# Hybrid attention and pooling block: numerator halves made further ahead, gate multiply and value-matrix product moved to later steps, PSUM banks shared

## The chip, the cores and the metric

One core of a Trainium2 chip runs the whole program. The metric is device time in microseconds (us) of one execution; the time before is the median of three runs. TensorE is called PE here (PEld is its weight load), VectorE DVE, ScalarE ACT, GpSimd POOL, and SP is SyncE, which issues the DMAs.

## What is computed

The reference is one layer of a hybrid block over 2048 latent tokens and 256 context tokens of width 1024. Cut to what matters here:

```python
h = _rms(x, norm_g) * (1 + scale) + shift          # hc likewise from ctx
u, uc = h @ w_in, hc @ w_in
q, k, v = _mla_qkv(u, ...)                          # 4 heads; rank-128 latent for keys and values
attn = softmax(q @ [kc, k].T * scale) @ [vc, v]     # 2048 queries, 2304 keys
br_a = silu(gate_a) * attn
br_p = silu(gate_p) * multiscale_pool(u, ...)
x_new = x + gate * (concat(br_a, br_p) @ w_out)
```

## The kernel before

The kernel works in three stages. A start-up and feature stage (to about 550 us) makes the modulated input, its projections, queries, keys, gates and the pooling branch. The attention stage (about 520 to 1100 us) follows. The output projection (L1012 to L1056) ends the kernel. Operands of matmuls are split in two halves, a rounded one and the rest, so that three products of halves stand for one product in full precision; `split` (L94) does so with an ACT copy and a subtraction.

**Attention.** The queries of a head come in blocks of 512, 16 blocks in all (`blocks`, L741), and a block is two row pairs p of 256 queries, 32 pairs. `scores(p, i)` (L757) handles 128 rows, i = 0 or 1: five chunks of keys (four of 512 in "A" banks, one of 256 in an "X" bank), five matmuls each; DVE takes the maximum of each chunk (L775), then ACT makes the exponentials (L793), a batch of five, and DVE transposes them in 32 by 32 squares into a W buffer (L796). `shuffle(p)` (L803) finishes the transpose with 16 DMAs on SP from that buffer to another W buffer (`PT[p]`). `pv(p)` (L845) takes nine steps: for each, `halves` (L850) makes the two halves of 256 numerators by 256 keys from `PT[p]`, ACT the first (L853), POOL the second (DVE for some; L855), in an M buffer, and `pv_mm` (L817) multiplies them with the latent values on PE (L821), six matmuls. Halves are made two steps ahead inside a pair; at a pair's beginning the first three are made at once. The last pair to end scores, 31, goes another way (`pv_last`, L829), with transposes on PE.

A block's two outputs lie in one "O" bank (L824). `latents(n)` (L892) copies it, split in two, to T buffers; `finish(n)` (L899) multiplies these with the value matrix (L903), multiplies with the gate (L905) and stores the branch (L908). `norm(n)` (L868) makes the reciprocals of the row sums: a PE transpose, two DMAs to DRAM (L879, L881), a DMA back that spreads them over the partitions (L884), the load of the gate (L886), and on POOL the product of the two (L887).

**What sets the order.** `attn` (L953) steps through the scores, ten steps a pair, and by a fixed rate lets `pv_all` (L929) do a step whenever it is due; LAG is 22 score steps:

```python
                    while done < (gc - LAG) * 9 / PER:
                        next(pg)
                        done += 1
```

So nine value steps go with ten score steps, and pair p's first value step stands in the program 13 score steps after the end of its scores. In `pv_all`, `norm(n)` comes at the start of a block's second pair, `latents` at its end, `finish` after step 2 of the next pair. From this program order a scheduler lays down a fixed order for each engine and for the SP queue, by priced durations; at run time each engine works through its list in order and waits at semaphores.

**Buffers.** SBUF buffers are given out by tag (L34): W 5, B 8, M 6, T 10, U 5. In the attention stage two W buffers hold transposes, two the shuffled numerators; M buffers hold the queries of the present and the next block, the value matrix and the halves. The query load of the next block (`load_q`, L735, L737), the key loads of the next head at two pairs (`load_k`, L712) and the loads of the output weights at pairs 28 to 30 (`load_wo`, L916) stand on the same SP queue. PSUM has 8 banks: A 5, X 2, O 1 (L78). "O" also serves a start-up sum (L297) and the pooling product (L648); X serves the last score chunk, transposes, `norm` and `finish`.

Of the kernel before, what the change touches and what calls it, by code (L numbers as in the profile page):

```python
# [10 lines left out]
F16 = mybir.dt.float16  # L11
# [13 lines left out]
NJ = NKEY // 128  # L25
# [28 lines left out]


LAG = 22
K_PF = (3, 5)
WO_AT = (1, 5, 11, 12, 12, 12, 13, 13)
CHUNKS = ((0, 512), (512, 512), (1024, 512), (1536, 512), (2048, 256))
# [4 lines left out]
def tile_hybrid_block(ctx: ExitStack, tc: tile.TileContext, x, c, cx, c_ctx, w_mod, b_mod, norm_g,  # L64
# [3 lines left out]
    x, cx, out = x[0], cx[0], out[0]  # L68
# [6 lines left out]
    sm = ctx.enter_context(tc.tile_pool(name="sm", bufs=3))  # L75
    ps = ctx.enter_context(tc.tile_pool(name="ps", bufs=1, space=bass.MemoryType.PSUM))
    dr = ctx.enter_context(tc.tile_pool(name="dr", bufs=1, space=bass.MemoryType.DRAM))
    PBUFS = {"A": 5, "X": 2, "O": 1}  # L78
    uid = [0]

    def nm(s):
# [3 lines left out]
    def st(tag, shape, dt=F32):  # L85
        return sb.tile([128] + list(shape), dt, tag=tag, bufs=BUFS[tag], name=nm(tag))

    def pt(tag, cols=512):
        return ps.tile([128, cols], F32, tag=tag, bufs=PBUFS[tag], name=nm("p" + tag))

# [200 lines left out]
    def mod_sum(b):  # L291

        wm, k0 = wms[b], KPS[b]
        mc = pt("X")
        mcv = mc[:, 0:8].rearrange("p (k s) -> p k s", s=2)
        if k0:
            mp = pt("O")  # L297
            for k in range(k0):
                nc.tensor.matmul(mp[0:2, :], lhsT=scv[:, k, :], rhs=wm[k // 2][:, k % 2, :], start=(k == 0),
                                 stop=(k == k0 - 1))  # L300
            mrow = st("T", [512])
            nc.scalar.copy(out=mrow[0:2, :], in_=mp[0:2, :])
        for i in range(4):
            if k0:
                nc.tensor.matmul(mcv[:, i, :], lhsT=mrow[0:2, i * 128:(i + 1) * 128], rhs=ident[0:2, 0:2],
                                 start=True, stop=(k0 == KT))
            if k0 < KT:
                nc.tensor.matmul(mcv[:, i, 0:1], lhsT=accs[b][:, i * 128:(i + 1) * 128], rhs=ones,
                                 start=(k0 == 0), stop=True)
        for i, o in ((0, 8), (1, 0)):  # L310
            nc.vector.tensor_copy(out=modc[:, b, 2 * i:2 * i + 2, :],
                                  in_=bmc[:, o + 2 * b:o + 2 * b + 2].unsqueeze(2).broadcast_to([128, 2, 2]))
        if k0 < KT:
            if k0:
                nc.vector.tensor_tensor(out=modc[:, b, :, 1], in0=mcv[:, :, 1], in1=modc[:, b, :, 1], op=ALU.add)
            mod_cols(b, 0, mcv[:, :, 0])
        else:
            for s in range(2):
                mod_cols(b, s, mcv[:, :, s])
# [275 lines left out]
    def feat(b):  # L595
# [6 lines left out]
        for g in range(H):  # L602
# [42 lines left out]
            n0 = a  # L645
            while n0 < e:
                n1 = e if e - n0 <= 512 else n0 + 260
                pp = pt("O")  # L648
                for n, (w, r) in enumerate(((wph, ph), (wph, pl), (wpl, ph))):
                    nc.tensor.matmul(pp[:, 0:n1 - n0], lhsT=w[:, g, :], rhs=r[:, n0:n1],  # L650
                                     start=(n == 0), stop=(n == 2))
                bo = st("T", [512])
                nc.vector.scalar_tensor_tensor(out=bo[:, 0:n1 - n0], in0=pp[:, 0:n1 - n0], scalar=psc[:, g:g + 1],
                                               in1=gp[:, n0 - 8:n1 - 8], op0=ALU.mult, op1=ALU.mult)
                nc.sync.dma_start(out=brd[1, g, :, t0 + n0 - 16:t0 + n1 - 16], in_=bo[:, 0:n1 - n0])
                n0 = n1
# [144 lines left out]
    PT = {}  # L801
# [21 lines left out]

    def out_bank(p):  # L824
        if p // 2 not in O:
            O[p // 2] = pt("O")
        return O[p // 2][:, (p % 2) * 256:(p % 2) * 256 + 256]

    def pv_last(p):  # L829
# [12 lines left out]
            pv_mm(p, o, j2, t)  # L842
            yield

    def pv(p):  # L845
        o = out_bank(p)
        src = PT.pop(p).rearrange("p q i j b -> p (q i) j b")
        ts = []

        def halves(j2):  # L850
            t = st("M", [2, 2, 8, 32], F16)
            s2 = src[:, :, 2 * j2:2 * j2 + 2, :].rearrange("p x j b -> p j x b")
            nc.scalar.activation(out=t[:, 0], in_=s2, func=AF.Copy)  # L853
            eng = nc.vector if j2 == 4 or (p == NP - 2 and j2 % 2) else nc.gpsimd
            eng.tensor_tensor(out=t[:, 1], in0=s2, in1=t[:, 0], op=ALU.subtract)  # L855
            ts.append(t)

        for j2 in range(NJ // 2):
            if j2 == 0:
                halves(0)  # L860
                halves(1)
            if j2 + 2 < NJ // 2:
                halves(j2 + 2)
            t = ts.pop(0)
            pv_mm(p, o, j2, t)
            yield

    def norm(n):  # L868

        h, qb = blocks[n]  # L870
        s4 = small(4, "s4")
        for i in range(4):
            nc.vector.reduce_sum(s4[:, i:i + 1], RS[n][i], axis=AX.X)
        nc.vector.reciprocal(out=s4, in_=s4)
        b = pt("X")
        nc.tensor.transpose(b[0:4, 0:128], s4, ident)
        rr = sm.tile([4, 128], F32, tag="rr", bufs=2, name=nm("rr"))
        nc.vector.tensor_copy(out=rr, in_=b[0:4, 0:128])
        nc.sync.dma_start(out=rvd[n].rearrange("(s n i r) -> s i n r", s=2, n=4, i=2)[0],  # L879
                          in_=rr[0:2].rearrange("i (n r) -> i n r", n=4))  # L880
        nc.sync.dma_start(out=rvd[n].rearrange("(s n i r) -> s i n r", s=2, n=4, i=2)[1],  # L881
                          in_=rr[2:4].rearrange("i (n r) -> i n r", n=4))
        rb = st("T", [512])
        nc.sync.dma_start(out=rb, in_=rvd[n].partition_broadcast(128))  # L884
        ga = st("T", [512])
        nc.sync.dma_start(out=ga, in_=gad[h, :, qb * 512:(qb + 1) * 512])  # L886
        nc.gpsimd.tensor_tensor(out=ga.rearrange("p (r n) -> p r n", n=16),  # L887
                                in0=ga.rearrange("p (r n) -> p r n", n=16),
                                in1=rb.rearrange("p (n r) -> p r n", n=16), op=ALU.mult)
        return ga  # L890

    def latents(n):  # L892

        o = O.pop(n)
        ol = [st("T", [512], F32R) for _ in range(2)]
        split(o, *ol)
        return ol
# [29 lines left out]
                yield  # L927

    def pv_all():  # L929
        ol = None  # L930
        for p in range(NP - 2):
            if p % 2:
                gau = norm(p // 2)
            for k, _ in enumerate(pv(p)):
                if k == 2 and ol:
                    finish(p // 2 - 1, ol, gaus)
                    ol = None
                yield
            if p % 2:
                ol, gaus = latents(p // 2), gau  # L940
        gau = norm(NP // 2 - 1)
        for k, _ in enumerate(pv_last(NP - 1)):
            if k == 2:
                finish(NP // 2 - 2, ol, gaus)
            yield
        yield from pv(NP - 2)
        finish(NP // 2 - 1, latents(NP // 2 - 1), gau)

    PER = 10
    WO_PF = (28, 29, 30)  # L950
# [154 lines left out]
```

## Time and profile before

| what | value |
|---|---|
| runs of the kernel before | 1283.88, 1286.53, 1290.29 us; median 1286.53 |
| the profiled execution, its own time | 1288.46 us |
| its span, first to last instruction | 1286.7 us |
| mean granted TensorE clock | 0.984 |
| PE, DVE, ACT, POOL busy | 1212.8, 831.1, 738.5, 562.1 us |

The span is one execution, from its first to its last instruction; times inside the trace count from the span's start. Idle time of an engine stands with what ended it, the releaser. The granted clock is a share of the full 2.4 GHz.

### The profile page before, as it was taken

How to read it: one execution, taken by the hardware profiler on the slowest of the kernel's cores; microseconds unless marked ns; L12 is line 12 of the kernel's file. 1: busy time of each engine (PE TensorE's matmuls, PEld its weight loads, DVE VectorE, ACT ScalarE, POOL GpSimd, SP SyncE). 2: the span in 40 equal slices, each digit the busy share in tenths (PEclk: the TensorE clock that was granted, in tenths of full speed). 3: DMA queues.
4: the chain of work that ended last, by engine and by line, in shares of the span. 5: the costliest groups of instructions: out<-in, count | busy, mean ns of one | idle time of the engine just before them, and what ended most of it. 6: DMA issues, size and time to landing. Idle time of an engine off the chain costs nothing.

```text
span 1286.7 us, 22292 instructions
## 1 busy us (share of the span) xinstructions
PE 1212.8 (94%) x7805; PEld 954.5 (74%) x7805; DVE 831.1 (65%) x1595; ACT 738.5 (57%) x1780; POOL 562.1 (44%) x638
## 2 busy tenths in 40 slices
PE   6799999999999998988999989999899999899998
PEld 3698989989899998755566655666556667688887
DVE  4966654765666555677788887888778887631211
ACT  5575665655575654466777767777667777511000
POOL 3645313524344342025566645654656654332221
PEclk9799999999999999999999999999999999999999
DMA  9446952574446547367877787777777778563321
GB/s 304 149 122 138 228 137 66 130 198 136 94 108 153 113 126 196 90 150 172 199 188 181 182 203 188 182 176 196 185 176 183 179 191 236 194 238 135 115 98 49
DMA packets 208213, 208.66 MB, mean 162 GB/s; under 512 B 92339, under 2 KB 168420, under 8 KB 207974
## 3 DMA queue, kind: packets, MB, share of 16 engines
q1 hardware_dynamic: 208102, 207.25, 62.0%
q8 instruction: 61, 1.00, 0.3%
q14 instruction: 50, 0.41, 0.1%
HBM read 98.50 MB, written 35.56 MB: 104 GB/s over the span
## 4 chain that ended last, share of the span: by engine, by line
PE 70%; DMA 11%; DVE 5%; SPq 5%; ACT 4%; issue 2%; POOL 2%; ACTq 0%; DVEq 0%; POOLq 0%
PE pA L588 17%; PE pA L1028 14%; PE pA L772 14%; PE pO L821 9%; PE pA L244 6%; SPq L811 3%; PE pA L519 2%; POOL M L855 2%; DMA M<-in_w_in_dram 2%; DMA rvd<-rr 2%; ACT M L853 2%; PE pX L772 1%; DMA W<-W 1%; DVE W L796 1%; PE pA L494 1%
## 5 line engine op out<-in xcount | busy, mean ns | idle before, releaser
L855 POOL TENSOR_TENSOR M<-W,M 128x512 f16<-128x512 f32 x244 | 291.3, 1218 | 193.3 <-ACT M L853 193.2
L772 PE MATMUL pA<-B,M 128*128 128x512 f16 x1280 | 303.9, 381 | 7.0 <-ACT T L793 3.6
L588 PE MATMUL pA<-W,B 128*128 128x256 f32 x2304 | 307.3, 287 | 0.1
L588 PEld LDWEIGHTS pA<-W,B 128*128 128x128 f32 x2304 | 290.2, 192 | 3.5 <-issue 0.9
L772 PEld LDWEIGHTS <-M 128*128 128x128 f16 x1600 | 156.4, 98 | 145.6 <-issue 7.3
L821 PE MATMUL pO<-M,B 128*128 128x256 f16 x1728 | 222.1, 276 | 21.2 <-POOL M L855 20.3
L793 ACT ACTIVATE T<-pA,nm,gm 128x512 f32<-128x512 f32 x248 | 189.6, 775 | 62.7 <-DVE nm L781 62.7
L821 PEld LDWEIGHTS <-B 128*128 128x128 f16 x1728 | 168.9, 99 | 71.6 <-issue 31.6
L796 DVE STREAM_TRANSPOSE W<-T 128x512 f32<-128x512 f32 x310 | 197.6, 647 | 25.2 <-ACT T L793 14.3
L853 ACT ACTIVATE M<-W 128x512 f16<-128x512 f32 x279 | 164.7, 632 | 84.3 <-PE pO L821 65.2
L775 DVE TENSOR_REDUCE mx<-pA 128x1 f32<-128x512 f32 x256 | 173.3, 680 | 37.8 <-PE pA L772 36.3
L1028 PE MATMUL pA<-W,B 128*128 128x512 f32 (+1 forms) x792 | 178.7, 386 | 4.8 <-ACT B L96 4.8
L1028 PEld LDWEIGHTS pA<-W,B 128*128 128x128 f32 x792 | 146.0, 189 | 34.2 <-ACT B L96 5.1
L1052 POOL TENSOR_TENSOR M<-T,M 128x512 f32<-128x512 f32 x30 | 38.7, 1294 | 113.6 <-DVE T L1049 109.4
L1049 DVE TENSOR_TENSOR T<-pA,M 128x512 f32<-128x512 f32 (+1 forms) x33 | 22.0, 673 | 101.1 <-PE pA L1028 101.1
L244 PE MATMUL pA<-B,W 128*128 128x448 f32 (+1 forms) x288 | 86.4, 371 | 0.0
L97 DVE TENSOR_TENSOR B<-M,B 128x1024 fp32r<-128x1024 f32 x48 | 61.5, 1282 | 32.1 <-ACT B L96 32.0
L96 ACT ACTIVATE B<-M 128x1024 fp32r<-128x1024 f32 (+2 forms) x53 | 55.3, 1044 | 45.2 <-DMA M<-in_w_in_dram 37.5
L887 POOL TENSOR_TENSOR T<-T,T 128x512 f32<-128x512 f32 x16 | 24.6, 1540 | 82.8 <-DMA T<-gad 49.5
L96 ACT ACTIVATE B<-B 128x2048 fp32r<-128x2048 f32 x8 | 15.3, 1918 | 75.2 <-DMA B<-brd 75.2
L244 PEld LDWEIGHTS pA<-B,W 128*128 128x128 f32 x288 | 54.7, 197 | 4.4 <-DVE T L275 0.9
L244 PE MATMUL pA<-W,W 128*128 128x448 f32 (+1 forms) x144 | 52.9, 369 | 0.0
(193 smaller groups left out, 1513.4 us busy)
## 6 DMA issues: line engine op xcount, KB each, us to landing
W<-W SPq DMA_DIRECT2D x496, 144.0 KB
M<-in_w_in_dram SPq DMA_DIRECT2D x48, 512.0 KB
B<-in_x_dram SPq DMA_DIRECT2D x16, 512.0 KB
B<-brd SPq DMA_DIRECT2D x8, 1024.0 KB
M<-in_x_dram SPq DMA_DIRECT2D x16, 512.0 KB
out_dram<-M SPq DMA_DIRECT2D x15, 512.0 KB
brd<-T SPq DMA_DIRECT2D x24, 256.0 KB
kd<-T SPq DMA_DIRECT2D x36, 128.0 KB
```

The costliest lines, as they stand in the source:

```text
L96: a = nc.scalar.activation(out=hi, in_=src, func=AF.Copy)
L97: (eng or nc.vector).tensor_tensor(out=lo, in0=src, in1=hi if hi.dtype == F16 else hi.bitcast(F32), op=ALU.subtract)
L244: nc.tensor.matmul(p[:, c0:NTOK], lhsT=a[:, kt, k * 128:(k + 1) * 128], rhs=b, start=(kt == 0 and n == 0), stop=(kt == KT - 1 and n == 2))
L588: nc.tensor.matmul(p[:, i * HB:(i + 1) * HB], lhsT=w[:, a, kt, :], rhs=b[:, kt, :], start=(m == 0), stop=(m == 23))
L772: nc.tensor.matmul(b[:, s0:s0 + sn], lhsT=q[:, a, c, p % 2, i], rhs=kt[ki][:, kc, o:o + sn], start=(m == 0), stop=(m == 4))
L775: nc.vector.reduce_max(mx[:, n:n + 1], b[:, :w], axis=AX.X)
L793: nc.scalar.activation(out=e[:, :w], in_=sp[n][:, :w], func=AF.Exp, bias=ng, scale=escale, accum_out=rs[:, n:n + 1])
L796: nc.vector.transpose(TP[p][:, :, i, j0:j1, :].rearrange("p q j b -> p j q b"), e[:, :w].rearrange("p (j q b) -> p j q b", q=4, b=32))
L821: nc.tensor.matmul(o, lhsT=V[0][:, j, a], rhs=t[:, c, jj], start=(j == 0 and m == 0), stop=(j == NJ - 1 and m == 2))
L853: nc.scalar.activation(out=t[:, 0], in_=s2, func=AF.Copy)
L855: eng.tensor_tensor(out=t[:, 1], in0=s2, in1=t[:, 0], op=ALU.subtract)
L1028: nc.tensor.matmul(bank[k, n, c0][:, 0:c1 - c0], lhsT=a[:, kt, k * 128:(k + 1) * 128], rhs=w[:, c, kt % 2, n * 512 + c0:n * 512 + c1], sta ...
```

## The change

Halves no longer use M buffers but a ring of eight slices in one W buffer (the fifth), made across the ends of pairs: at each value step `halves` fills a queue up to six, the present step's and five ahead, as far as `shuffle` of the pair has been issued in the program. The ninth slice holds the spread reciprocals. `norm` is cut in two: the loads stay where they were (at the end of a block's first pair), the multiply with the gate (`gated_norm`) comes after step 4 of the next block's first pair, and `finish` after its step 6 in place of 2. For the last block, `norm` comes after `pv_last(31)`, and its gate multiply at the very end. The O bank is gone; X has three banks, and outputs, the start-up sum and the pooling product take theirs from X.

```diff
+AHEAD, RING = 5, 8
+FIN_AT = (4, 6)
...
-    PBUFS = {"A": 5, "X": 2, "O": 1}
+    PBUFS = {"A": 5, "X": 3}
...
-            mp = pt("O")
+            mp = pt("X")
...
-                pp = pt("O")
+                pp = pt("X")
...
-            O[p // 2] = pt("O")
+            O[p // 2] = pt("X")
...
-    def pv(p):
-        o = out_bank(p)
-        src = PT.pop(p).rearrange("p q i j b -> p (q i) j b")
-        ts = []
-
-        def halves(j2):
-            t = st("M", [2, 2, 8, 32], F16)
-            s2 = src[:, :, 2 * j2:2 * j2 + 2, :].rearrange("p x j b -> p j x b")
+    aux, hq = [], []
+    todo = [(p, j2) for p in range(NP - 1) for j2 in range(NJ // 2)]
+
+    def halves(ahead=AHEAD):
+        while todo and len(hq) < ahead and todo[0][0] in PT:
+            p, j2 = todo.pop(0)
+            if not aux:
+                a = st("W", [4608])
+                aux.extend(a[:, i * 512:(i + 1) * 512] for i in range(9))
+            n = p * (NJ // 2) + j2
+            t = aux[n % RING].bitcast(F16).rearrange("p (c j x b) -> p c j x b", c=2, j=2, x=8)
+            s2 = PT[p].rearrange("p q i j b -> p j (q i) b")[:, 2 * j2:2 * j2 + 2]
             nc.scalar.activation(out=t[:, 0], in_=s2, func=AF.Copy)
             eng = nc.vector if j2 == 4 or (p == NP - 2 and j2 % 2) else nc.gpsimd
             eng.tensor_tensor(out=t[:, 1], in0=s2, in1=t[:, 0], op=ALU.subtract)
-            ts.append(t)
-
+            hq.append((p, j2, t))
+
+    def pv(p):
+        o = out_bank(p)
         for j2 in range(NJ // 2):
-            if j2 == 0:
-                halves(0)
-                halves(1)
-            if j2 + 2 < NJ // 2:
-                halves(j2 + 2)
-            t = ts.pop(0)
+            halves(AHEAD + 1)
+            ph, jh, t = hq.pop(0)
             pv_mm(p, o, j2, t)
             yield
+        PT.pop(p)
...
-        rb = st("T", [512])
+        rb = aux[RING]
         nc.sync.dma_start(out=rb, in_=rvd[n].partition_broadcast(128))
         ga = st("T", [512])
         nc.sync.dma_start(out=ga, in_=gad[h, :, qb * 512:(qb + 1) * 512])
+        return rb, ga
+
+    def gated_norm(rb, ga):
         nc.gpsimd.tensor_tensor(out=ga.rearrange("p (r n) -> p r n", n=16),
...
     def pv_all():
-        ol = None
-        for p in range(NP - 2):
-            if p % 2:
-                gau = norm(p // 2)
-            for k, _ in enumerate(pv(p)):
-                if k == 2 and ol:
-                    finish(p // 2 - 1, ol, gaus)
-                    ol = None
+        last = None
+        for p in [*range(NP - 2), NP - 1, NP - 2]:
+            for k, _ in enumerate(pv_last(p) if p == NP - 1 else pv(p)):
+                if last and k == FIN_AT[0]:
+                    gau = gated_norm(*last[2])
+                if last and k == FIN_AT[1]:
+                    finish(*last[:2], gau)
+                    last = None
                 yield
-            if p % 2:
-                ol, gaus = latents(p // 2), gau
-        gau = norm(NP // 2 - 1)
-        for k, _ in enumerate(pv_last(NP - 1)):
-            if k == 2:
-                finish(NP // 2 - 2, ol, gaus)
-            yield
-        yield from pv(NP - 2)
-        finish(NP // 2 - 1, latents(NP // 2 - 1), gau)
+            if p % 2 == 0 and p < NP - 2 or p == NP - 1:
+                nrm = norm(p // 2)
+            else:
+                last = p // 2, latents(p // 2), nrm
+        finish(*last[:2], gated_norm(*last[2]))
```

## Rows read from the trace of the kernel before

**Rows 1.** The page, busy time, share of the span and instructions of each engine

```profile
PE 1212.8 (94%) x7805; PEld 954.5 (74%) x7805; DVE 831.1 (65%) x1595; ACT 738.5 (57%) x1780; POOL 562.1 (44%) x638
```

**Rows 2.** Stretches: length; PE, PEld, DVE, ACT, POOL busy; PEclk, DMA share, GB/s

```profile
603.00:1055.00 452.00, 428.58 (x2756) 272.68 (x2756) 368.16 (x754) 329.19 (x768) 263.41 (x221) 0.99 0.77 187
...
845.60:878.77 33.17, 32.48 (x212) 20.85 (x212) 27.96 (x59) 25.24 (x60) 20.46 (x18) 1.00 0.77 184
878.77:917.11 38.34, 34.09 (x213) 21.46 (x213) 28.50 (x59) 25.59 (x60) 20.08 (x18) 0.96 0.78 189
```

**Rows 3.** Waits of PE, 550 to 1100 us: us in total, times, longest

```profile
PE pO L821 <- POOL M L855: 20.3, 14, 4.1
PE pX L903 <- ACT T L96: 9.6, 14, 0.7
PE pA L1028 <- ACT B L96: 4.8, 1, 4.8
...
PE pO L821 <- ACT M L853: 0.9, 1, 0.9
```

**Rows 4.** One of five stretches at the lower clock, columns as in rows 2

```profile
904.40:907.81 3.41, 2.99 (x14) 1.92 (x14) 0.00 (x0) 1.24 (x2) 3.41 (x4) 0.50 0.98 230
```

**Rows 5.** Timeline of PE and POOL in the longer block: start, us, instruction, [idle before]

```profile
904.82 2.72 PE L821 MATMUL pO<-M,B 128*128 128x256 f16 x12 [3.56 <-POOL M L855]
...
902.13 1.53 POOL L887 TENSOR_TENSOR T<-T,T 128x512 f32<-128x512 f32 x1 [7.60 <-DMA W<-W]
903.62 5.59 POOL L855 TENSOR_TENSOR M<-W,M 128x512 f16<-128x512 f32 x5
```

**Rows 6.** Timeline of the SP queue in the same block

```profile
888.94 0.59 SPq L712 DMA_DIRECT2D B<-kd  x1
...
890.61 0.36 SPq L881 DMA_DIRECT2D rvd<-rr  x1
896.11 0.34 SPq L884 DMA_DIRECT2D T<-rvd  x1
```

**Rows 7.** Timeline of PE at the end of a block

```profile
841.48 3.44 PE L821 MATMUL pO<-M,B 128*128 128x256 f16 x30
845.60 0.74 PE L903 MATMUL pX<-T,M 128*128 128x512 f32 x2 [0.69 <-ACT T L96]
```

**Rows 8.** Waits of the SP queue, 520 us to the end

```profile
SPq L735 <- PE pO L821: 60.2, 13, 7.1
...
SPq L811 <- POOL M L855: 15.3, 11, 5.6
```

**Rows 9.** Pair 17: last transposes, shuffle, two stretches (as rows 2), first halves

```profile
837.96 1.03 DVE L796 STREAM_TRANSPOSE W<-T 128x512 f32<-128x512 f32 x2
...
844.60 10.74 SPq L811 DMA_DIRECT2D W<-W  x16
...
844.60:858.00 13.40, 12.71 (x83) 8.00 (x82) 11.46 (x23) 11.04 (x28) 5.99 (x6) 1.00 0.91 222
858.00:860.00 2.00, 2.00 (x11) 0.94 (x10) 1.90 (x6) 0.94 (x2) 2.00 (x2) 1.00 0.16 59
...
864.21 1.67 ACT L853 ACTIVATE M<-W 128x512 f16<-128x512 f32 x3
```

**Rows 10.** Pair 17: PE's last score group, first and last exponential of its second batch

```profile
834.00 0.71 PE L772 MATMUL pX<-B,M 128*128 128x256 f16 x5
...
834.28 0.78 ACT L793 ACTIVATE T<-pA,nm,gm 128x512 f32<-128x512 f32 x1 [0.54 <-DVE nm L781]
...
837.32 0.57 ACT L793 ACTIVATE T<-pX,nm,gm 128x256 f32<-128x256 f32 x1
```

**Rows 11.** Timeline of ACT in the tail

```profile
1097.12 1.91 ACT L96 ACTIVATE B<-B 128x2048 fp32r<-128x2048 f32 x1 [5.77 <-DMA B<-brd]
...
1105.10 2.18 ACT L853 ACTIVATE M<-W 128x512 f16<-128x512 f32 x4
```

More of the change, by code (lines that the diff above doesn't have):

```diff
@@ L855, in halves @@
             eng.tensor_tensor(out=t[:, 1], in0=s2, in1=t[:, 0], op=ALU.subtract)
-            ts.append(t)
+            hq.append((p, j2, t))
+    def pv(p):
+        o = out_bank(p)
         for j2 in range(NJ // 2):
-            if j2 == 0:
-                halves(0)
-                halves(1)
-            if j2 + 2 < NJ // 2:
-                halves(j2 + 2)
-            t = ts.pop(0)
+            halves(AHEAD + 1)
+            ph, jh, t = hq.pop(0)
+            assert (ph, jh) == (p, j2)
             pv_mm(p, o, j2, t)
             yield
+        PT.pop(p)
     def norm(n):
```

## The prediction

> **What bounds the kernel now.** I read the page first: TensorE is busy 1212.8 of 1286.7 us, 94%, and no other engine passes 65% [rows 1]. A busy share can mean slow matmuls, so I next took the stretches of the attention stage. From 603 to 1055 us, thirteen blocks of two row pairs, PE is busy 428.58 of 452 us and VectorE, next, 368 [rows 2]. A block without a stall lasts 33.17 us with PE busy 32.48; one with a stall lasts 38.34 with PE busy 34.09 [rows 2]. Thirty value-product matmuls in a row take 3.44 us [rows 7], 0.11 each, for 256 columns, and 256 columns at the 2.4 GHz level are 0.107 us. So PE streams when it is busy, and in this stage the idle time of PE is what there is to win. The list of its waits from 550 to 1100 us names that time: 20.3 us in 14 waits of the value product for POOL's lower halves, 9.6 us in 14 waits of the value-matrix product (L903) for ACT's split, 4.8 us once before the output projection, 0.9 us for ACT's halves [rows 3].
>
> One more cost is not in that list. At five places after 550 us the granted clock is 0.50 of full speed, the 1.2 GHz level, for 3.41 us [rows 4]. Four of them lie at waits of the value product (beginning at 586.97, 764.46, 904.40 and 941.95 us), the fifth at the 4.8 us gap (1098.96): at each PE had just sat idle, for 3.56 us in rows 5, for 4.8 in rows 3. At half speed 3.41 us lose 1.7. The two blocks of rows 2 bear this out: 5.2 us apart, of which 3.56 is the stall [rows 5] and 1.61 more PE busy time.
>
> Where the waits come from: POOL stands at the gate multiply (L887) for 7.60 us until its loads have landed, and the lower halves queue behind it; PE's wait of 3.56 us ends as soon as they run [rows 5]. The gate's loads are late because SyncE issues a key load of 1.2 MB at 888.94, then the reciprocals' write at 890.61, and reads them back only at 896.11 [rows 6]. The L903 wait has another cause: at a block's end PE has one bank for the output, "O", so nothing of the next block may start before ACT has copied it; 0.69 us, the same each time [rows 3, 7].
>
> **The change part by part.** It removes no arithmetic and adds none: as many halves, gate multiplies, value-matrix products and DMAs. All of the sum is waits.
>
> *Gate multiply to step 4 of the next pair.* The loads of rows 6 then have more than a pair, some 16 us, to land; POOL no longer stands there. *Halves five steps ahead.* PE finds them made at a pair's start, where it now finds two at most; POOL's 1.1 us per half [rows 5] lie beside PE's 0.65 us per step and its scores. Together these take the 20.3 us; the ends are 0, if something else is late at the same place, and 20.3. I take 20.3 for the waits named, and charge what may be late next below. The 0.9 us I leave: it is the first pair, where the halves come straight after the first shuffle.
>
> *The clock.* With four waits gone, four drops go: 4 x 1.7 = 6.8 us; ends 0 and 6.8.
>
> *O in the X banks, value-matrix product to step 6.* The next block's output gets a bank while the old one is copied, and L903 stands six steps later, when its input is long there: 9.6 us. Against it: scores, norm transposes and L903 itself share what is left, two X banks as before, but one for the moment in which two outputs live. That moment is ACT's copy and VectorE's subtraction after it, about twice the 0.69 us. No row shows it; its cost lies between 0 and a wait like the present one at each of 16 ends, 11 us. I take 5, between them, since the row it is nearest to is 0.69 but the scores need the bank only once in 8 us. The same sharing in the start-up and feature stages (L297, L648) I cost at nothing, as the total of banks is the same and feature matmuls hide the product; if that cover fails, some three waits of 0.69 us either way, 2 us.
>
> *Ring in the fifth W buffer.* M buffers are freed: query loads wait 60.2 us in 13 waits on SyncE for an M buffer that PE must release, and shuffles wait 15.3 us for POOL to finish reading the target [rows 8]. Both lie in front of the shuffle. Transposes of pair 17 end at 838.99, its shuffle starts at 844.60 [rows 9]; this 5.6 us goes, but gains nothing by itself, as the halves run only at 864.21 [rows 9]. It is the lead that the earlier halves use up. The reciprocals' load goes to the ring's ninth slice and waits for the gate multiply five steps before: nothing. In the tail the output weights' first tile needs a buffer of the attention; 0 to 1 us, hidden behind the last pairs, and I put 0.
>
> *The tail.* PE sits idle 4.8 us, and the clock falls for 1.7 more, until ACT splits the first branch tile at 1097.12, while halves of pair 30 are made only at 1105.10 [rows 11]. Five of its nine steps can now be ready before: 6.5 us; ends 0 and 6.5.
>
> *What is late next: the shuffle's landing.* From its first issue to the last packet are 13.4 us [rows 9], where the DMA share falls from 0.91 to 0.16 at 858.0. PE's last score group of pair 17 starts at 834.00, its exponentials end at 837.9 [rows 10], the transposes at 838.99. With 13.4 us, ACT's half (1.67 for three, 0.6 [rows 9]) and POOL's (1.1) the first halves are there 20.1 us after that group; PE's value product is written 13 score steps after it, 1.3 pairs of 16.2 us, or 21.1. About 1 us is left. A key or weight load on SyncE makes the reciprocals take 5.5 us [rows 6], and with them the shuffle behind; nine pairs have such a load. If a stall like the present 3.56 us [rows 5], less that 1 us, came back at each, 9 x 2.5 = 23 us; if SyncE's earlier start absorbs it, 0. I take 8, nearer the lower end, as the waits of rows 8 go.
>
> Sum: -20.3 - 6.8 - 9.6 - 6.5 + 5 + 8 = -30.2 us. Against the profiled execution's own 1288.46 us (span 1286.7) that is 1258.3; the median of the runs is 1.9 us below that execution, so 1256.4, and I say **1257 us**.
>
> **Rivals.** *1. The landing takes half of it.* PE's waits at pair starts return as waits for the shuffle in about half of the size, with their clock drops: 13.5 us of the 27.1 return, and no more than half of the tail's gain comes. 30.2 less 13.5 less 3 leaves some 14: 1272, within 1268 to 1280. For it: 1 us of slack [rows 9, 10] and DMA engines at 0.77 of the stretch [rows 2]. Against: SyncE loses its waits of rows 8.
>
> *2. Nothing comes of it, 1281 to 1292.* The lead of five isn't there, because halves cannot precede a landing that comes within a step of their use, and another engine sets the pace. VectorE at 0.81 and PE's weight loads at 0.60 of the stretch [rows 2] speak for a look at this, the 0.11 us spacing [rows 7] against it. The Trainium skill, page "Perfetto Trace Analysis", section "Identifying the Most-Contended Engine", says that matmul busy time doesn't measure how near PE is to its limit and asks for the LDWEIGHTS share instead. By that rule PE had headroom here, the gaps were no measure, and the time would be this rival's; the trace disagrees by the spacing of rows 7.
>
> *3. Slower: ACT blocked.* ACT works in a fixed order. If the first half of a pair stands in front of the next pair's second batch of exponentials, ACT waits there for the landing with scores ready behind it, their banks stay full and PE runs out of scores. The ring is then: exponentials' end, transposes 1.1, landing 13.4, half 0.6, exponentials 3.6 (834.28 to 837.9): 18.9 us a pair at least with issue and semaphores, against 17.4 in the stretch of rows 2 (452/26). Over 31 pairs: 1.5 x 31 = 46, about 1333. Against a pair without stalls (16.3) it loses 2.6, so it decides from about half of the pairs on; there and above, 1293 to 1335. For it: the batch would be ready at 16.3 - 3.6 = 12.7 us after the last, the half at 14.5 plus. Against: the order is laid down with a price for transfers, and it need not put a half there.
>
> **How the numbers follow.** Forecast 0.60 (1243 to 1268: all 43 us down to 20 of them); rival 1 0.17; rival 2 0.09; rival 3 0.14. 0.5% is 6.4 us, about what a measurement of this kernel can tell from no change. Faster by more, below 1280: 0.60 + 0.17 = 0.77; same 0.09; slower 0.14. The range runs from 1243, all waits gone and nothing late, to 1288, which takes in rival 1 and part of rival 2.
>
> **What would show it.** Right: no wait of the value product for POOL above 1 us, none of L903 for ACT, no clock drop after 560 us but at the end of the attention, POOL's gate multiply without a wait, query loads on SyncE without one, blocks of 32.5 to 33.5 us. Rival 1: PE waits for POOL or ACT at pair starts, with a shuffle's DMA as their releaser. Rival 3: ACT's half waits for W<-W several us with exponentials behind it, VectorE and PE idle. Wrong altogether: blocks of 33 us without gaps, yet no shorter total, or a longer feature stage before 550 us.

## The result, and the profile after

The changed kernel takes 1301.63 us (median of 4 runs, 1299.89 to 1306.2); the kernel before, beside it, 1285.91. The ratio is 1.0123, interval [1.0085, 1.0161]: slower by 1.2%, where 1257 us was forecast. The profiled execution took 1299.89 us, span 1298.0. Line numbers have moved: scores are L774, exponentials L795, transposes L798, the shuffle L813, the value product L823, halves L861 and L863, the gate multiply L898, the value-matrix product L914.

The page's busy times hardly change, as no arithmetic did [rows 1]:

```profile
PE 1213.6 (93%) x7805; PEld 953.6 (73%) x7805; DVE 839.5 (65%) x1595; ACT 730.1 (56%) x1780; POOL 550.6 (42%) x638
```

The loss lies in the attention. From the 101st score matmul to the last it takes 537.3 us where it took 522.8, 14.4 more; the rest of the kernel is 3.1 us shorter. The two stretches, before and after (columns as in rows 2):

```profile
555.04:1077.88 522.84, 491.23 (x3142) 310.90 (x3140) 421.69 (x866) 377.92 (x882) 298.69 (x251) 0.99 0.76 184
553.93:1091.20 537.27, 497.94 (x3168) 312.82 (x3167) 429.57 (x863) 370.24 (x884) 301.93 (x255) 0.99 0.74 178
```

PE's idle time (length less busy time) is 39.3 us in place of 31.6, and its busy time is 6.7 us longer at the same clock. Some 3 us of that are 26 more value matmuls that now fall into the stretch; the record does not show what the rest is. Ends of matmuls are modelled in the profile, so a part of each stall may count as busy.

A block without a load and one with:

```profile
819.49:853.92 34.43, 33.01 (x212) 20.79 (x212) 28.84 (x58) 24.72 (x61) 20.34 (x18) 1.00 0.74 176
745.47:785.27 39.80, 34.67 (x213) 21.24 (x213) 29.01 (x58) 24.73 (x61) 19.89 (x18) 0.96 0.73 183
```

They are 1.3 and 1.5 us longer than before [rows 2]. PE's waits from 550 to 1100 us, to be read beside rows 3:

```profile
PE pX L823 <- POOL W L863: 33.0, 40, 4.0
PE pA L774 <- ACT T L795: 3.2, 2, 2.1
PE pX L823 <- ACT W L861: 2.2, 3, 1.2
```

The wait of the value-matrix product for ACT's split is gone, as forecast. The waits for POOL's lower halves have grown, from 20.3 us in 14 to 33.0 in 40: short ones in every block, and five long ones, 16.0 us of the 33.0. A long one, on POOL and PE (start, us, instruction, idle before):

```profile
765.21 1.52 POOL L898 TENSOR_TENSOR T<-T,W 128x512 f32<-128x512 f32 x1 [4.22 <-DMA W<-rvd]
```
```profile
767.89 0.82 PE L823 MATMUL pX<-W,B 128*128 128x256 f16 x6 [4.01 <-POOL W L863]
```

POOL still stands at the gate multiply, 4.22 us here and 3.38 in the block where it was 7.60 [rows 5], though the program has it 14 value steps later (the nine of the block's second pair and five of the next). The laid-down order put it in the middle of the lower halves of the block's second pair; that it was put where its loads were expected is likely, but not shown.

What every block has in common is seen on ACT at pair 17. The shuffle's issue on the SP queue, then ACT, then DVE's last transposes of pair 18:

```profile
849.28 10.82 SPq L813 DMA_DIRECT2D W<-W  x16
```
```profile
861.03 0.78 ACT L795 ACTIVATE T<-pA,nm,gm 128x512 f32<-128x512 f32 x1 [4.13 <-DVE nm L783]
...
863.72 1.67 ACT L861 ACTIVATE W<-W 128x512 f16<-128x512 f32 x3 [1.82 <-DMA brd<-T]
865.30 0.76 ACT L795 ACTIVATE T<-pA,nm,gm 128x512 f32<-128x512 f32 x1
...
867.57 0.56 ACT L795 ACTIVATE T<-pX,nm,gm 128x256 f32<-128x256 f32 x1
```
```profile
867.13 1.61 DVE L798 STREAM_TRANSPOSE W<-T 128x512 f32<-128x512 f32 x3
```

ACT makes one exponential of pair 18's second batch, then stands 1.82 us for pair 17's numerators, which landed 14 us after the shuffle's first issue (the row names another DMA that ended at about that time, a branch store), makes three halves, and only then the other four exponentials, whose input had been ready as long as the first one's. The Trainium skill, page "PSUM — Partial Sum Buffer", section "Engine vs sequencer instructions", says that ScalarE's queue is strictly first in, first out; the 865.30 behind the 863.72 agrees. PE has moved as well:

```profile
862.60 1.24 PE L774 MATMUL pA<-B,M 128*128 128x512 f16 x5
864.40 0.38 PE L823 MATMUL pX<-W,B 128*128 128x256 f16 x2 [0.56 <-ACT W L861]
864.62 0.71 PE L774 MATMUL pX<-B,M 128*128 128x256 f16 x5
865.64 0.81 PE L823 MATMUL pX<-W,B 128*128 128x256 f16 x6 [0.31 <-POOL W L863]
```

Pair 17's first value step stands right at the landing, with score chunks (the five matmuls of one chunk of keys) behind it. Counted in score chunks from its place in the program (22 chunks plus 10/9 per step), an odd pair's first value step began 10 chunks late before and begins 0 late now.

The fixed order on ACT around pair 18's exponentials (E18.0 and E18.1, two batches of five; h17 the halves of pair 17, copy the output's):

```
before   E18.0 x5, h16 x3, E18.1 x5, h16 x3, E19.0 x5, h17 x4, E19.1 x5, h17 x5
changed  E18.0 x5, E18.1 x1, h17 x3, E18.1 x4, h17 x6, E19.0 x5, E19.1 x5, copy, h18 x9
```

### The profile page after: what moved, and what is told of

Read it like the earlier page. It is cut to its first block, busy times and chain, and to the rows that moved or that the text cites. A ratio compares the mean times of both kernels' runs of the same rounds, so it can differ in the third digit from the quotient of the medians.

```text
span 1298.0 us, 22438 instructions
## 1 busy us (share of the span) xinstructions
PE 1213.6 (93%) x7805; PEld 953.6 (73%) x7805; DVE 839.5 (65%) x1595; ACT 730.1 (56%) x1780; POOL 550.6 (42%) x638
## 4 chain that ended last, share of the span: by engine, by line
PE 66%; DMA 11%; SPq 7%; DVE 7%; issue 4%; POOL 3%; ACT 2%; POOLq 0%; ACTq 0%; DVEq 0%
PE pA L590 18%; PE pA L1036 13%; PE pA L774 13%; PE pX L823 7%; SPq L813 6%; PE pA L246 6%; POOL W L863 3%; PE pA L521 2%; DMA W<-W 2%; DMA rvd<-rr 2%; DVE W L798 2%; DMA M<-in_w_in_dram 1%; DMA W<-rvd 1%; DVE mx L777 1%; PE pX L232 1%
## 5 line engine op out<-in xcount | busy, mean ns | idle before, releaser
L863 POOL TENSOR_TENSOR W<-W,W 128x512 f16<-128x512 f32 x244 | 282.8, 1190 | 261.9 <-ACT W L861 169.5
L774 PE MATMUL pA<-B,M 128*128 128x512 f16 x1280 | 310.3, 385 | 6.5 <-ACT T L795 6.4
L590 PE MATMUL pA<-W,B 128*128 128x256 f32 x2304 | 303.6, 286 | 0.0
L795 ACT ACTIVATE T<-pA,nm,gm 128x512 f32<-128x512 f32 x248 | 189.6, 772 | 145.6 <-DVE nm L783 145.6
L823 PE MATMUL pX<-W,B 128*128 128x256 f16 x1674 | 225.8, 274 | 36.0 <-POOL W L863 33.0
L774 PEld LDWEIGHTS <-M 128*128 128x128 f16 x1600 | 157.6, 99 | 137.0 <-issue 17.6
L823 PEld LDWEIGHTS <-B 128*128 128x128 f16 x1728 | 168.2, 98 | 106.9 <-issue 57.2
L798 DVE STREAM_TRANSPOSE W<-T 128x512 f32<-128x512 f32 x310 | 196.9, 647 | 51.1 <-ACT T L795 45.9
L861 ACT ACTIVATE W<-W 128x512 f16<-128x512 f32 x279 | 150.4, 632 | 22.3 <-DMA W<-W 8.8
L98 ACT ACTIVATE B<-B 128x2048 fp32r<-128x2048 f32 x8 | 15.4, 1924 | 80.1 <-DMA B<-brd 77.8
L236 ACT ACTIVATE T<-pX,shc,ac 128x256 f32<-128x256 f32 x72 | 36.1, 570 | 23.2 <-DVE shc L291 10.3
```

The lines of the kernel that those rows point to most:

```text
L98: a = nc.scalar.activation(out=hi, in_=src, func=AF.Copy)
L590: nc.tensor.matmul(p[:, i * HB:(i + 1) * HB], lhsT=w[:, a, kt, :], rhs=b[:, kt, :], start=(m == 0), stop=(m == 23))
L774: nc.tensor.matmul(b[:, s0:s0 + sn], lhsT=q[:, a, c, p % 2, i], rhs=kt[ki][:, kc, o:o + sn], start=(m == 0), stop=(m == 4))
L795: nc.scalar.activation(out=e[:, :w], in_=sp[n][:, :w], func=AF.Exp, bias=ng, scale=escale, accum_out=rs[:, n:n + 1])
L798: nc.vector.transpose(TP[p][:, :, i, j0:j1, :].rearrange("p q j b -> p j q b"), e[:, :w].rearrange("p (j q b) -> p j q b", q=4, b=32))
L823: nc.tensor.matmul(o, lhsT=V[0][:, j, a], rhs=t[:, c, jj], start=(j == 0 and m == 0), stop=(j == NJ - 1 and m == 2))
```

## The experiments

Each ratio is to the kernel before on the same chip, with its 95% interval. The ranges in us of the expectations start from 1286 us, while the kernel before took 1288 to 1293 us on the chips of these runs, so the ratios decide. In runs 1 to 4 theory A was the shuffle's landing, theory B the sharing of the X banks.

**Run 1, the ring alone; run 2, the banks alone; run 3, the later gate multiply and value-matrix product alone; run 4, all but the shared banks.** Runs 1 to 3 put one part of the diff into the kernel before. Run 4 is the changed kernel with

```diff
-    PBUFS = {"A": 5, "X": 3}
+    PBUFS = {"A": 5, "X": 2, "O": 1}
```
and "O" again at the three places.

> Of the change only the ring: halves up to five steps ahead across pair ends in the fifth W buffer; gate multiply, value-matrix product and the O bank as before. Theory A (the halves cannot come before the shuffle has landed; with the M buffers out of the way ACT makes all nine at the landing, the value steps move up to right behind it, and each block pays about 1.2 us): slower than before by 10 to 18 us, 1296 to 1304, PE's waits for POOL at steps 0, 3 and 5 of nearly every block. Theory B (the loss comes from sharing the X banks): within 5 us of before or faster, 1260 to 1291.

> Of the change only the banks: outputs, start-up sum and pooling product in three X banks, everything else as before. Theory A: nearly nothing, -5 to +5 us (1281 to 1291); the 0.69 us waits of the value-matrix product stay, because it is placed at step 2. Theory B: slower by 10 to 18 us, 1296 to 1304, with PE's scores waiting for a bank.

> Of the change only the later steps: gate multiply after step 4 of the next pair and value-matrix product after step 6; halves in M buffers two ahead and the O bank as before. Theory A: the scheduler still puts the gate multiply on POOL where its loads land, so the five stalls of the blocks with key or weight loads stay; the 0.69 us wait moves from the value-matrix product to the value steps, as there is one O bank: -5 to +5 us, 1281 to 1291. Theory B says the same of this one. If the step on POOL really moved, the 20 us of stalls and their clock drops would go: 1258 to 1268.

> The changed kernel, but with the O bank of its own again (X two). Theory A: as slow as the changed kernel or slower, since the next block's output must wait for the copy again: 1298 to 1312. Theory B: back to the time before or faster, 1270 to 1290.

Measured: run 1 1277.93 us, 0.9893 [0.9865, 0.9921]; run 2 1297.54, 1.0044 [1.0022, 1.0065]; run 3 1289.17, 0.9985 [0.9967, 1.0003]; run 4 1271.40, 0.9845 [0.9816, 0.9873]. This looked like theory B: a bank of its own for the output turned 1.2% slower into 1.6% faster. But banks alone cost only 0.4%, where theory B asked for 10 to 18 us, the later multiply and product alone nothing that can be told, and run 4's ACT differs too. At the same place:

```profile
848.45 0.77 ACT L795 ACTIVATE T<-pA,nm,gm 128x512 f32<-128x512 f32 x1
...
851.28 1.67 ACT L861 ACTIVATE W<-W 128x512 f16<-128x512 f32 x3 [1.97 <-DMA W<-W]
...
854.36 0.56 ACT L795 ACTIVATE T<-pX,nm,gm 128x256 f32<-128x256 f32 x1
```

Two exponentials are done ahead of the halves (847.68 and 848.45), three stand behind. With the bank, the order had moved by one.

**Runs 5 to 8, orders forced.** Runs 5 and 6 hold value steps on PE behind the score chunk written last before them, with shared and own bank: run 5 the steps that its edit names, run 6 all steps of nearly all pairs. Runs 7 and 8 hold the gate multiply behind a lower half, own and shared bank. In runs 5 and 6 theory A is another one: the order of the value steps.

```diff
+                if jj == m == 0 and p % 2 and 0 < p < NP - 2 and j2 in (0, 1, 2, 7):
+                    order(scored[-1], mm.ins, "the value step stays behind the scores")
```
```diff
+        if n < NP // 2 - 2:
+            order(lows[2 * n + 2, 3].ins, a.ins, "the gate multiply stays behind the halves")
```

> The changed kernel, banks shared as it has them, with one thing more: in the odd pairs the value steps 0, 1, 2 and 7 may not stand ahead of the score chunk written last before them. On TensorE they move back by 1 to 4 score chunks from where the changed kernel has them. Theory A (order): the sharing costs time because a bank that is free at once lets the order put an odd pair's value steps a chunk too early, where TensorE then waits for POOL's lower halves with scores behind it; then this kernel comes close to the one with an own bank, 1268 to 1283 us, blocks of 32.6 to 33.2 us without the four waits of 0.2 to 0.5 us at the starts of odd pairs. Theory B (room): the score chunks lack a bank while an output sits in one; the order doesn't matter and it stays at 1295 to 1306 us, blocks of 34 us or more.

> The changed kernel with a bank of its own for the output (as in the run before) and no value step ahead of the score chunk written last before it: value steps 4 to 6 of each pair move back by 2 to 3 chunks. Theory A: TensorE meets halves that are made longer ago, the waits of 0.3 to 0.8 us at the steps 2 and 3 of even pairs (13.7 us in 31 waits) shrink by half or more and the time falls by 5 to 10 us, to 1261 to 1267. Theory B has no reason for a change: 1268 to 1275, since the waits come from POOL's pace of 1.1 us per lower half and not from where the steps stand. A third outcome, slower than 1278, would say that the later steps hold up the next pair's scores or the output bank.

> The changed kernel with a bank of its own for the output, and the gate multiply held behind POOL's lower half of step 3 of the next pair, so that POOL no longer stands at it for the reciprocals with lower halves behind. If POOL's stand of 2.6 to 3.3 us at the gate multiply in blocks with a load (seven waits, 13.5 us) still reaches TensorE, the time falls to 1258 to 1266. If it is hidden there, as TensorE's longest wait for POOL of 0.8 us in that kernel suggests, it stays within 1266 to 1276. The order of TensorE changes with it (value steps up to 4 chunks earlier); by theory A that alone can cost up to 15 us, 1276 to 1288.

> The changed kernel, banks shared, with the gate multiply held behind POOL's lower half of step 3 of the next pair. The five waits of TensorE of 2.5 to 4.0 us in blocks with a load, with their clock drops (four times 1.7 us), are 16.0 + 6.8 = 23 us of the changed kernel. If they come from POOL standing at the gate multiply, they go: 1278 to 1290. If the price of sharing lies in the order of the value steps in every block (1.2 us in each of 16), 15 to 20 us of it stay: not under 1278. If POOL's stand is not their cause: 1296 or more.

Measured: run 5 1300.64, 1.0073 [1.0046, 1.0101]; run 6 1293.71, 1.0016 [0.9991, 1.0042]; run 7 1290.64, 0.9998 [0.9982, 1.0013]; run 8 1265.18, 0.9799 [0.9764, 0.9833]. Runs 5 to 7 missed their gains, run 5 inside theory B's range. But run 8 beat its own gain, and with shared banks: theory B fell. What sorts them is ACT's order, which each added edge had changed. In runs 5 to 7 seven halves stand ahead of a whole batch of five exponentials in every other odd pair (run 6: idle 5.34 us at 893.87 for the landing). In run 8 an odd pair's halves stand behind all five.

**Run 9, ACT's order alone; run 10, the same with an own bank; run 11, run 8 with the changed kernel's order back on ACT; run 12, runs 8 and 9 together.**

```diff
+            if True and p + 1 < NP - 1 and (p + 1, 1) not in exps:
+                break
...
+            if (p + 1, 1) in exps:
+                order(exps[p + 1, 1].ins, up.ins, "the halves stay behind the exponentials")
```

> The changed kernel, banks shared, the gate multiply where it was, with one thing more: a pair's halves stand on ScalarE behind the five exponentials of the next pair's second batch. In the changed kernel the first three halves of each odd pair stand behind the first of these five, and four exponentials wait with them for the shuffle's landing: trend to landing 14.0 us, half and four exponentials 5.0 us, 19.0 us for that pair, 15.4 for the other, 34.4 a block. Theory C (ScalarE blocked): that order is the loss; with it gone pairs take 16.3 to 17.2 us each, blocks 32.6 to 33.5, and the time is 1258 to 1276 us. Theory G (gate multiply): the loss is POOL's stand at the gate multiply, which stays; the five waits of TensorE of 2.5 to 4.0 us and their clock drops stay and the time is not under 1282. Theory B (bank): not under 1295.

> The same order of ScalarE with a bank of its own for the output. In the kernel with the own bank three exponentials stood behind an odd pair's first halves, not four, and pairs took 18.3 to 18.9 and 14.2 to 14.5 us in turn. Theory C: what is left of that wait goes, 1256 to 1270 us, and the difference between an own and a shared bank shrinks from 30 us to under 10. Theory B: an own bank is still better than a shared one by 20 us or more. Neither: TensorE's waits of 0.7 us for ScalarE's copy of the output, as in the kernel before, come back and make it slower than 1275.

> The kernel with the gate multiply behind POOL's lower halves (1265 us) with the changed kernel's order put back on ScalarE: the first three halves of each odd pair behind the first of the five exponentials of the next pair's second batch, four exponentials behind them. Theory C: most of the gain of that run came with ScalarE's order, which moving the gate multiply had changed too; it is lost again, pairs of 19 and 15.4 us in turn, 1283 to 1303 us. Theory G: the gain came from POOL; it stays at 1262 to 1272.

> Both: the gate multiply behind POOL's lower half of step 3, and all halves of a pair behind the five exponentials, banks shared. In the run with the gate multiply alone moved, ScalarE had one exponential left behind three halves in even pairs and none in odd ones. Theory C: nearly the same, 1255 to 1266 us; if the two costs are separate and add up, it is the fastest of all and under run 9 by what POOL's stand still costs there, 0 to 10 us. Slower than 1272 would say that the order of the value steps on TensorE, which differs in all these kernels, weighs more than either.

Measured: run 9 1261.84, 0.9756 [0.9732, 0.9780]; run 10 1300.28, 1.0065 [1.0037, 1.0093]; run 11 1283.44, 0.9911 [0.9880, 0.9941]; run 12 1261.02, 0.9742 [0.9714, 0.9771]. Run 9 takes 3.6% off the changed kernel with one rule on ACT's order; PE's value steps moved with it, those of an odd pair from 0 to 5 chunks late. ACT there, PE's waits from 550 to 1100 us, and POOL at a gate multiply:

```profile
841.14 0.78 ACT L795 ACTIVATE T<-pA,nm,gm 128x512 f32<-128x512 f32 x1 [4.53 <-DVE nm L783]
...
844.72 4.79 ACT L864 ACTIVATE W<-W 128x512 f16<-128x512 f32 x9
```
```profile
PE pA L774 <- ACT T L795: 12.0, 15, 2.2
PE pX L823 <- POOL W L868: 6.6, 7, 1.5
```
```profile
884.73 1.52 POOL L903 TENSOR_TENSOR T<-T,W 128x512 f32<-128x512 f32 x1 [3.10 <-DMA W<-rvd]
```

The halves run in one go without a wait. POOL still stands 3.10 us at the gate multiply, but PE's longest wait for it is 1.5: theory G's five long waits went while their cause stayed. Run 11 is 1.1% above run 8; by its ratio (1275 on 1286 us) it lies between theories C and G. So with early halves POOL's stand costs too: run 11 has nearly the changed kernel's order on ACT and PE, the gate multiply aside, and is 2.1% below it. With late halves the stand costs 0.1% (run 12 against run 9, within the intervals).

Run 10 was the third outcome of its expectation:

```profile
PE pX L919 <- ACT T L98: 21.5, 15, 2.2
```

With an own bank, the output's copy stood behind eight halves on ACT and held the bank for all of them.

**Runs 13 and 14, the bank alone.** Run 9's rule, and the copy ahead of the next pair's halves; ACT's order is the same in both from pair 4 to pair 28, the bank is own in 13 and shared in 14. **Run 15**: the changed kernel with the three halves one exponential earlier.

```diff
+            if p % 2 == 0 and p // 2 - 1 in copies:
+                order(copies[p // 2 - 1], up.ins, "the halves stay behind the copy of the output")
```

> Halves behind the exponentials as in run 9, and the output's copy on ScalarE ahead of the next pair's halves, with a bank of its own for the output. Run 10 had the copy behind eight halves, and TensorE waited 21.5 us in 15 waits of the value-matrix product for it. Theory C with the copy as run 10's cause: 1262 to 1276 us. If an own bank as such is what made run 10 slow: 1285 or more.

> The same order of ScalarE as run 13, instruction for instruction in the attention, with the banks shared. The only difference of the two is the bank, and with it one value step of TensorE a block. What sharing is worth by itself is this run less run 13: by the prediction's terms -9.6 + 5 = -5 us; theory B says +20 or more. By theory C this one is at 1256 to 1268.

> The changed kernel with the first three halves of each odd pair one exponential earlier on ScalarE: all five exponentials of the next pair's second batch stand behind them, where four do in the changed kernel, and three in the kernel with an own bank. Theory C: an exponential takes 0.72 us; the pair that waits takes 0.7 us more, 19.7 us, and the time is 1304 to 1325. If the position of the halves on ScalarE didn't matter: 1297 to 1304, as the changed kernel.

Measured: run 13 1253.15, 0.9709 [0.9693, 0.9724]; run 14 1253.96, 0.9709 [0.9679, 0.9739]; run 15 1313.88, 1.0175 [1.0152, 1.0197]. Sharing the banks is worth nothing either way. Runs 13 and 14 are the fastest kernels here, 2.9% below the one before, and both fell below their expected ranges. With five exponentials behind the halves it is worse than with four, as expected:

```profile
870.75 1.67 ACT L863 ACTIVATE W<-W 128x512 f16<-128x512 f32 x3 [6.85 <-DMA T<-gad]
872.32 0.76 ACT L795 ACTIVATE T<-pA,nm,gm 128x512 f32<-128x512 f32 x1
```

**Runs 16 and 17, ACT and PE apart.** In all these runs PE's value steps had moved with ACT's halves. Run 16 is run 15 with the value steps of odd pairs held behind the scores; run 17 is run 14 with the next score chunk held behind an odd pair's first three value steps. (Run 16's edit holds the second exponential and not the first, but ACT's order came out as in run 15 from pair 4 to pair 28.) On PE the first three steps of an odd pair moved by 2 to 4 chunks, later in run 16 and earlier in run 17.

> Run 15's order of ScalarE (three halves of each odd pair ahead of all five exponentials), with the odd pairs' value steps on TensorE held behind the score chunk written last before them, which puts the first three of them 2 to 3 score chunks later than in run 15. In all runs so far the two orders changed together. Theory C1 (the loss is ScalarE standing at the landing with exponentials behind it): no gain, 1305 to 1325 us. Theory C2 (the loss is TensorE reaching the odd pairs' value steps too early, before POOL's lower halves, with score chunks behind them): most of it goes, 1262 to 1285.

> Run 14's order of ScalarE (no half ahead of an exponential), with the score chunk that follows held behind the first three value steps of each odd pair, so that these stand 3 to 4 score chunks earlier on TensorE than in run 14 and within one chunk of where the changed kernel has them. Theory C1: ScalarE never stands at the landing with exponentials behind it, little is lost, 1254 to 1272 us. Theory C2: TensorE stands at these steps as in the changed kernel, and longer, since the halves come 3 us later: 1285 to 1315.

Measured: run 16 1296.12, 1.0074 [1.0048, 1.0099]; run 17 1281.60, 0.9953 [0.9932, 0.9973]. Neither C1 nor C2 alone (in brackets, by how many chunks an odd pair's first value step is late on PE):

| ratio to the kernel before | value steps late on PE | early on PE |
|---|---|---|
| no half ahead of an exponential on ACT | 0.9709 (run 14; 5) | 0.9953 (run 17; 1) |
| three halves ahead of five exponentials | 1.0074 (run 16; 2) | 1.0175 (run 15; -1) |

Within a row ACT's order is the same, so the quotients are PE's: 2.5% (upper row) and 1.0%. Within a column PE's steps are not equally late, so 3.8% (late) and 2.2% are not ACT's share alone. The nearest pair for that is run 16 against run 17 (2 chunks and 1): ACT's early halves cost 1.2% there, though run 16's steps are the later ones. So both orders cost time, and how much each does by itself is not settled. PE's waits in 550 to 1100 us are of two kinds: in run 17 many short ones for POOL's halves (second row; run 14 in the first), in run 16 for ACT's exponentials, which free the score banks (third row):

```profile
PE pX L823 <- POOL W L872: 4.2, 8, 0.7
```
```profile
PE pX L825 <- POOL W L876: 19.0, 29, 0.9
```
```profile
PE pA L774 <- ACT T L796: 27.6, 16, 3.2
```

## Why the prediction was wrong

**What failed is the step "What is late next: the shuffle's landing", priced at 8 us, and with it the choice against rival 3.** The step found 1 us left between the first halves and their use, and charged waits for nine pairs with loads only. That 1 us is a misread row. The score group at 834.00 [rows 10] is already the next pair's: the exponentials that begin at 834.28 need the maximum over all of pair 17's groups, the last of which VectorE took at 833.12, and nm, the scaled maximum that they subtract, was made from it at 834.03, before that group ended. The last group of pair 17 is the third of the four in the first row, begun at 831.84 (a group takes 1.08 us). Kernel before:

```profile
829.68 4.48 PE L772 MATMUL pA<-B,M 128*128 128x512 f16 x20
```
```profile
833.12 0.69 DVE L775 TENSOR_REDUCE mx<-pA 128x1 f32<-128x512 f32 x1 [0.21 <-PE pA L772]
...
834.03 0.21 DVE L781 TENSOR_SCALAR nm<-nm,gm 128x1 f32<-128x1 f32 x1
```

By the step's own sum the first halves are then there 22.3 us after that group, against 21.1: 1.2 us short, in a block without a load. In the changed kernel pair 17's first value step, which ran as soon as its half was there, began 22.8 us after the last score group (841.63 to 864.40):

```profile
841.63 1.24 PE L774 MATMUL pA<-B,M 128*128 128x512 f16 x5
```

With a ring to fill, the scheduler put the halves and value steps of every odd pair straight at the landing, on ACT with four exponentials behind, on PE with score chunks behind.

Rival 3 had a part of this mechanism: the half that waits for the landing on ACT with exponentials behind it. Its 18.9 us for a pair that waits stand against 19.5 from pair 17's shuffle to pair 18's (849.28 to 868.80), and it was to decide "from about half of the pairs on", which is what the odd pairs are. I gave it 0.14 because the order "need not put a half there". That was a hope about a program that could not be seen, not a row: rows 9 showed halves 6 us behind the landing in the old order, and nothing showed that they would stay there. But rival 3 was not right as it stood. ACT stood 1.82 us and not several, PE waited only 3.2 us for exponentials and stood at the value steps instead, and the next pair took 15.4 us (868.80 to 884.18), so that a block lost 1.3 us and not 2.6. That 1301.63 lies in its 1293 to 1335 is partly luck: 2.1% of the time is POOL's gate multiply, which it did not count, and without that the ratio is 0.9911 (run 11).

In run 9, where the halves do stay behind the exponentials, the profiled execution takes 1262.8 us against the sum's 1258.3. The total is near, the terms are not: run 9's 12.0 us of waits for exponentials stand in no term.

Step by step, changed kernel first, then run 9:

- *Gate multiply and halves, -20.3.* Failed: 33.0 us of waits for POOL, and POOL still stands at the gate multiply in blocks with a load. In run 9 6.6 us, POOL standing all the same. What the stand costs hangs on the lead of the halves over PE: 2.1% with early halves (run 11), 0.1% with late ones (run 12).
- *The clock, four drops, -6.8.* Failed with it: five stretches of 3.41 us at the 1.2 GHz level between 560 and 1110 us, as many as before [rows 4]. In run 9 one, at 1067.97 in the tail.
- *Value-matrix product, -9.6.* The wait is gone, but PE's first idle time of a block moved on to its fourth value step, in every block (13 such waits of 0.74 us from 600 to 1100 us, 9.6 us again):

```profile
853.92 1.25 PE L823 MATMUL pX<-W,B 128*128 128x256 f16 x10 [0.74 <-POOL W L863]
```

- *Output in the X banks, +5, ends 0 and 11.* Runs 13 and 14: 1253.15 and 1253.96, no difference beyond their intervals; the row nearest to it was right and 5 too high. Run 13 shows that the 9.6 us needed no sharing: with the copy ahead of the halves the own bank gives them too (L923 waits for the copy once, 0.4 us, from 550 to 1100).
- *The ring's buffer, 0.* Right as a price: the query loads on the SP queue wait 23.5 us (L737, three releasers) where they waited 60.2 [rows 8], and the shuffle's wait for POOL is down from 15.3 us to 0.6:

```profile
SPq L813 <- POOL W L863: 0.6, 2, 0.4
```

- *The tail, -6.5.* From the last score matmul to the first of the output projection 16.6 us against 20.8, so 4.3 of it came.

My second theory, that the shared banks were the loss (runs 1 to 4), fell in the same manner: the edit did one thing and the order of two engines another. Shown is that the time comes back when the halves are held behind the exponentials that are ready, with the value steps moving along, and that it goes again when either is put back early. Why the scheduler chose the early places is open, and giving the landing more room by a larger LAG was not tried.

## What to carry to other kernels

Where a scheduler lays down fixed orders, list what each edit does to the order of every engine before reading its time as the edit's own: here one bank, one edge or one ring shifted three ACT instructions by one exponential or more, and with each shift went 0.5 to 2.8% of the time. Work that waits for a long transfer belongs behind the work that is ready, on every engine that it passes, and a margin that falls out of the written order has to be pinned. A margin of 1 us in 21 needs a second row that shows to which pair the first belongs. When a rival's mechanism is at hand and only its place in the order is unknown, give it the chance of a coin, not of a mishap.

## What was not expected of the hardware

A wait of PE of several us was not always followed by the lower clock. The rows, from the changed kernel, are the 3.41 us from the end of a wait of 3.12 us (909.69), of one of 2.67 us (945.80) and of one of 2.49 us (1086.87); the clock is the number behind POOL's count:

```profile
909.69:913.10 3.41, 3.41 (x22) 2.09 (x22) 1.48 (x4) 0.00 (x0) 3.28 (x3) 1.00 0.93 231
...
945.80:949.21 3.41, 3.41 (x12) 1.61 (x12) 0.24 (x2) 0.00 (x0) 3.27 (x3) 0.54 0.98 231
...
1086.87:1090.28 3.41, 3.41 (x22) 2.10 (x22) 1.16 (x3) 0.41 (x2) 3.27 (x3) 1.00 0.98 228
```

So the 1.7 us that the prediction put on each long wait is not due at every one: two of the five long waits went without. The short waits of 0.74 us, one in each block, were followed by none.
